# Input and latent weights of a hybrid attention block packed by K tile, multiplied K outermost over six feature tiles

## Chip, core and metric

The kernel runs on one core of a Trainium2 chip. The time is the device time of one execution in microseconds (us). Three timed runs of the kernel before took 450.87, 450.98 and 451.32 us; the median is 450.98 us.

## The reference

The block takes x with 256 positions and 1024 features, normalizes it, and multiplies it by one wide matrix `w_in`. The first 704 columns of `w_in` give the latents: 384 for the queries, 256 for keys and values, and 64 for a shared rotary key.

```python
h = rmsnorm(x, attn_norm[l])
proj = h @ w_in[l]
q_lat = proj[..., OFF_QLAT:OFF_KVLAT]
kv_lat = proj[..., OFF_KVLAT:OFF_KPE]
k_pe = proj[..., OFF_KPE:OFF_MOBA]
qkv_b = proj[..., OFF_MOBA:OFF_GATE]
gates = jax.nn.sigmoid(proj[..., OFF_GATE:] + b_gate[l])
```

Two attention branches follow (MLA from the latents, and MoBA from `qkv_b`, which for 256 positions is causal attention within one block). They are merged by the gates and projected. Then comes a gated feed-forward part with a short causal convolution, and a last norm. All of it is float32.

## The kernel before

The kernel makes every float32 product on TensorE of three float32r matmuls. Each operand is split into a part rounded to float32r (the high part, written by ScalarE) and the rest (the low part, written by VectorE), and the three are high by high, high by low and low by high (`mm3`, `split`). A matmul of a feature tile multiplies a 128x128 tile of weights by 256 positions.

The weights stream through SBUF once. `unit_plan` lists the loads in the order of their use; a unit is 128 partitions by 2048 float32, 1 MB. `weights` takes the next unit: a raw tile, a high tile and a low tile, each from a ring of three, the load on SyncE's queue (SP), and the split. The queue is in order: a load that waits for its raw tile holds up those behind it.

The order of instructions on each engine is set by a planner. All instructions are recorded in the order of the computation; `Program.emit` then gives each engine the oldest instruction whose operands are there by a simple model of times. Loads on SP keep their recorded order. What stands within `P.together()` stays together.

The first stage computes six feature tiles of 128 columns, the latents (the sixth is the rotary key, doubled). It goes like this:

- TensorE runs ten matmuls on a zeroed tile `warm`, and SP loads the input norm's weights `prm[:, :KT]`.
- The transposed input comes from its own array `xT` and unit `("lat", 0)`, two feature tiles, from `wpack`. Both are loaded in five pieces each, in turn: K tile 0, K tile 1, then 2 and 3, 4 and 5, 6 and 7. A piece of one K tile has 256 columns, 1 KB in a row.
- For each of the eight K tiles ScalarE scales and rounds the input (`XH`) and rounds the weights (`whi`), and VectorE writes the rests (`XL`, `wlo`), all 256 columns wide. TensorE multiplies K outermost over the two feature tiles, 6 matmuls a K tile, 48 in all.
- Units `("lat", 1)` and `("lat", 2)` follow in `proj_pair`: two feature tiles each, all K tiles of one tile and then of the next, 48 matmuls each. Each unit has its own PSUM bank of the ring `mm_bank` (three banks). Unit 1 is loaded in four pieces, unit 2 in two.
- After each unit, `keep_latents` copies its bank to SBUF and squares it, both on ScalarE.

The value projection of MoBA (`proj_tokens("v", 0, ...)`, units `v` 0 and 1) is the next work of TensorE, and then units `v` 2 and 3. Between the two the input is loaded again by rows (`b8`), and its norm's factor is worked out from it.

Of the kernel before, what the change touches and what calls it, by code (L numbers as in the profile page):

```python
"""Hybrid MLA + MoBA block with a ConvFFN on one core.

Every float32 product on the tensor engine is three float32r passes: both operands are split
into a part rounded to float32r and the exact rest (hi*hi + hi*lo + lo*hi, summed in PSUM).
Weights stream through SBUF once, in the order of their use, and are split on the way.
Activations stay on chip, features on partitions where they are contracted next.

MoBA: SEQ equals MOBA_BLOCK, so there is one block, none lies in the past of any query, every
selected score is masked and what is left is causal attention within the block.
"""  # L10
# [28 lines left out]
# columns of the small parameters  # L39
# [4 lines left out]
def unit_plan():  # L44
    """The weights in the order of their use: (kind, index)."""
    plan = [("lat", 0), ("lat", 1), ("lat", 2)]
# [17 lines left out]
SIZE = {"mqk": 3 * 384 + 2 * 256}  # the others have UNIT columns  # L64


def pack_weights(w_in, w_uq, w_ukv, w_o_mla, w_o_moba, w_out, w_up, w_down):
    """Layout alone: each unit as [128 rows of K, column group, K tile, columns of the group]."""
# [9 lines left out]
    # rotated halves lie 64 partitions apart: [x1, x1, x2, x2]  # L78
# [3 lines left out]
    for kind, i in PLAN:  # L82
        if kind == "lat":
            u = tiles(w_in, lat_cols[256 * i : 256 * i + 256], 128 if i else 256)
# [34 lines left out]
def rope_tables():  # L119
    """cos and the signed sin by [row, position]; rows r and r + 64 are a rotated pair."""  # L120
# [11 lines left out]
def constants():  # L132
    """Tables that depend on shapes alone: rope, the identity, the causal mask of a block, the
    rows of the first and of the second head in a pair's rotated tile."""
    p = np.arange(128)
    mask = np.where(p[None, :] <= p[:, None], 0.0, -1e30).astype(np.float32)
    sel = np.stack([(p // 32) % 2 == 0, (p // 32) % 2 == 1], axis=1).astype(np.float32)
    return np.ascontiguousarray(
        np.concatenate([*rope_tables(), np.eye(128, dtype=np.float32), mask, sel], axis=1)
    )  # L140


class Program:
    """Instructions, recorded in the order of the computation and emitted in the order of a
    simple model of the engines: each engine takes the oldest of its instructions whose operands
    are there. What reads or writes the same part of a tile keeps its order, and so do functions
    of the scalar engine with tables of their own."""

    LATENCY = {"tensor": 0.8}  # others 0.15
    DMA_LATENCY = 1.6  # L150

    def __init__(self, nc):
        self.nc = nc
        self.ops = []  # [engine, cost, calls, dependencies]
        self.users = {}  # tile -> [(op, region, writes)]
# [8 lines left out]
    def together(self):  # L164
        """Instructions of one engine that stay together."""
# [42 lines left out]
    def emit(self):  # L208
# [16 lines left out]
        for _ in range(n):  # L225
            best = None
            for e, js in open_ops.items():
                if not js:
                    continue
                if e == "sync":  # a queue  # L230
                    js = [j for j in js if j == min(loads)]
                    if not js:
                        continue
# [14 lines left out]
            else:  # L248
                free[e] = end = start + cost
            for a in after[j]:  # L250
# [19 lines left out]
def region(ap):  # L270
    """Partitions and elements of a tile that an access covers."""
# [5 lines left out]
def price(engine, method, args, kw):  # L277
    """Microseconds, about."""
    n = max(int(np.prod(a.shape[1:])) for a in list(args) + list(kw.values())
            if hasattr(a, "offset"))  # L280
    if engine == "tensor":
# [3 lines left out]
        return passes * max(0.107, 0.0025 + args[0].shape[1] / 2400)  # L285
    if engine == "scalar":
# [12 lines left out]
def hybrid_block(ctx: ExitStack, tc: tile.TileContext, xT, x, par, con, fnorm, wpack, out):  # L299
# [9 lines left out]
    class Ring:  # L309
        """Tiles that take turns."""  # L310
# [32 lines left out]
    units = iter(range(len(PLAN)))  # L343

    def weights(kind, i, *cuts):
        """The next unit's two parts, split in pieces that end at the cuts."""
# [5 lines left out]
        for a, b in zip((0, *cuts), cuts) if u < 3 else ((0, n),):  # L352
            sp.dma_start(raw[:, a:b], wpack[u, :, a:b])
# [22 lines left out]
    first = T("first", [4])  # L376
    act.activation(first, mhalf, AF.Exp)
    o = av_bank()
    for _ in range(10):
# [3 lines left out]
    sp.dma_start(prm[:, :KT], par[:, :KT])  # L383
    xraw, w0 = raws(), raws()
    wv = [his(), los()]
    next(units)
    xh, xl = T("XH", [KT, S], F32R), T("XL", [KT, S], F32R)
    for ks in ((0,), (1,), (2, 3), (4, 5), (6, 7)):
        c = slice(S * ks[0], S * ks[-1] + S)
        sp.dma_start(xraw[:, c], xT[:, c])  # L390
        sp.dma_start(w0[:, c], wpack[0, :, c])
    for k in range(KT):
        c = slice(S * k, S * k + S)
        g = prm[:, P_AN + k : P_AN + k + 1]
        act.activation(xh[:, k], xraw[:, c], AF.Copy, scale=g)
        act.copy(wv[0][:, c], w0[:, c])
        dve.scalar_tensor_tensor(xl[:, k], xraw[:, c], g, f32(xh[:, k]), op0=ALU.mult,
                                 op1=ALU.subtract)
# [506 lines left out]
```

## Time and profile before

| | |
|---|---|
| timed runs | 450.87, 450.98, 451.32 us, median 450.98 |
| span of the profiled execution | 450.0 us; its own time is not listed apart from the span |
| TensorE matmuls busy | 439.0 us (98%), 3302 |
| weight loads (PEld) | 415.4 us (92%) |
| VectorE | 356.7 us (79%) |
| ScalarE | 274.8 us (61%) |
| mean DMA rate over the span | 182 GB/s |
| TensorE's mean granted clock | 0.992 |

The span is the time from the first to the last instruction of the profiled execution. Times in rows of the trace are in us from its start. All instructions of the kernel go through a recorder and so bear its line (L242); a row is told apart by engine and by tiles, written as out<-in. `XH` and `XL` are the input's two parts, `whi` and `wlo` the weights', `raw` a loaded unit, `mm`, `av` and `sc` PSUM banks, `gate` the tile that holds the latents in the first stage, `warm` the zeroed tile.

### The profile page before, as it was taken

What the parts mean: (1) busy time and instruction counts of PE and PEld (TensorE: products, weight loads), DVE (VectorE), ACT (ScalarE), POOL (GpSimd) and SP (SyncE); (2) the same over time, 40 slices, a digit from 0 to 9 for tenths busy, and PEclk for the clock granted to TensorE, in tenths of its full rate; (3) what the DMA queues carried; (4) which work ended last, traced back from release to release, by engine and by line L of the source; (5) the groups of instructions that cost most, each with busy time, mean ns of one, the idle gap of its engine ahead of it and who ended that gap; (6) DMA issues with size and microseconds to landing.
All of it is one profiled execution on the core that took longest, in us unless ns stands there. A gap on an engine that the chain in (4) does not pass through costs nothing.

```text
span 450.0 us, 8134 instructions
## 1 busy us (share of the span) xinstructions
PE 439.0 (98%) x3302; PEld 415.4 (92%) x3302; DVE 356.7 (79%) x548; ACT 274.8 (61%) x475; POOL 10.8 (2%) x26
## 2 busy tenths in 40 slices
PE   7999999999999999999999999999999999999993
PEld 4988999999999999999998899999999999999982
DVE  3767998888987988793788568997887797797764
ACT  5786446546554766877765558765565565565523
POOL 0010300000000000000000010000000000000002
PEclk9999999999999999999999999999999999999998
DMA  6994745455254434240288454375555555556002
GB/s 197 399 402 162 263 155 184 178 183 181 90 185 165 137 124 182 93 174 17 105 340 302 188 188 137 144 288 197 190 201 203 192 205 198 197 192 233 2 1 93
DMA packets 13861, 81.77 MB, mean 182 GB/s; under 512 B 1664, under 2 KB 2560, under 8 KB 5120
## 3 DMA queue, kind: packets, MB, share of 16 engines
q1 hardware_dynamic: 13824, 81.25, 49.9%
q8 instruction: 26, 0.43, 0.4%
q14 instruction: 11, 0.09, 0.1%
HBM read 80.20 MB, written 1.05 MB: 181 GB/s over the span
## 4 chain that ended last, share of the span: by engine, by line
PE 96%; DMA 1%; SPq 1%; ACT 1%; POOL 1%; issue 0%; DVE 0%; POOLq 0%; ACTq 0%
PE mm L242 69%; PE av L242 14%; PE sc L242 12%; DMA raw<-in_wpack 1%; SPq L242 1%; POOL smalls L242 1%; ACT tb L242 0%; DVE gate L242 0%; ACT B L242 0%; POOLq L900 0%; ACT whi L242 0%; POOLq L242 0%; ACTq L242 0%
## 5 line engine op out<-in xcount | busy, mean ns | idle before, releaser
L242 ACT CAST whi<-raw 128x1024 fp32r<-128x1024 f32 (+3 forms) x158 | 152.3, 978 | 86.0 <-PE mm L242 70.3
L242 DVE TENSOR_TENSOR wlo<-raw,whi 128x1024 fp32r<-128x1024 f32 (+3 forms) x158 | 175.8, 1129 | 34.6 <-ACT whi L242 33.9
L242 PE MATMUL mm<-XH,whi 128*128 128x256 f32 x656 | 184.4, 281 | 1.8 <-ACT whi L242 1.8
L242 PE MATMUL mm<-XH,wlo 128*128 128x256 f32 x656 | 182.7, 278 | 0.0
L242 PE MATMUL mm<-XL,whi 128*128 128x256 f32 x656 | 182.5, 278 | 0.0
L242 PEld LDWEIGHTS mm<-XH,whi 128*128 128x128 f32 x656 | 124.3, 189 | 2.7 <-ACT whi L242 2.3
L242 PEld LDWEIGHTS mm<-XL,whi 128*128 128x128 f32 x656 | 124.2, 189 | 0.5
L242 PEld LDWEIGHTS mm<-XH,wlo 128*128 128x128 f32 x656 | 124.4, 190 | 0.2 <-DVE wlo L242 0.2
L242 DVE SCALAR_TENSOR_TENSOR tb<-ta,prm,tb 128x255 f32<-128x255 f32 x88 | 40.4, 480 | 2.2 <-ACT tb L242 0.7
L242 ACT ACTIVATE tb<-ta,prm 128x256 f32<-128x256 f32 x44 | 24.3, 595 | 3.8 <-DVE ta L242 3.8
L242 ACT ACTIVATE e<-sc,smalls 128x128 f32<-128x128 f32 (+1 forms) x32 | 13.3, 419 | 12.6 <-DVE smalls L242 11.7
L242 DVE TENSOR_TENSOR ta<-ta,tb 128x256 f32<-128x256 f32 (+1 forms) x35 | 16.9, 484 | 2.2 <-ACT ta L242 0.7
L242 ACT CAST qh<-ta 128x256 fp32r<-128x256 f32 (+1 forms) x26 | 11.4, 437 | 11.8 <-DVE ta L242 11.7
L242 DVE TENSOR_TENSOR ta<-mm,rbc 128x512 f32<-128x512 f32 x22 | 15.2, 689 | 4.2 <-PE mm L242 4.2
L242 PE MATMUL mm<-YBH,whi 128*128 128x256 f32 x64 | 18.1, 283 | 0.0
L242 PE MATMUL mm<-YBH,wlo 128*128 128x256 f32 x64 | 17.7, 277 | 0.0
L242 PE MATMUL mm<-VH,whi 128*128 128x256 f32 x64 | 17.7, 277 | 0.0
L242 PE MATMUL mm<-YBL,whi 128*128 128x256 f32 x64 | 17.7, 277 | 0.0
L242 PE MATMUL mm<-VL,whi 128*128 128x256 f32 x64 | 17.7, 276 | 0.0
L242 PE MATMUL mm<-VH,wlo 128*128 128x256 f32 x64 | 17.7, 276 | 0.0
L242 PE MATMUL sc<-whi,ql 128*128 128x512 f32 x44 | 17.3, 394 | 0.0
L242 PE MATMUL av<-whi,ql 128*128 128x512 f32 x44 | 17.3, 394 | 0.0
(167 smaller groups left out, 735.1 us busy)
## 6 DMA issues: line engine op xcount, KB each, us to landing
raw<-in_wpack SPq DMA_DIRECT2D x66, 1024.0 KB, 4.8
raw<-in_wpack SPq DMA_DIRECT2D x4, 832.0 KB, 4.2
raw<-in_wpack SPq DMA_DIRECT2D x7, 256.0 KB, 6.6
raw<-in_wpack SPq DMA_DIRECT2D x2, 512.0 KB, 5.2
B<-in_x SPq DMA_DIRECT2D x1, 1024.0 KB, 10.0
gate<-in_x SPq DMA_DIRECT2D x1, 1024.0 KB, 4.8
raw<-in_xT SPq DMA_DIRECT2D x3, 256.0 KB, 6.1
cst<-in_con SPq DMA_DIRECT2D x1, 641.0 KB, 11.1
```

Source lines behind the costliest of these rows:

```text
L242: getattr(getattr(self.nc, e), method)(*args, **kw)
```

## The change

The transposed input and the latents' weights are packed together by K tile. Units `("lat", 0..2)` and the array `xT` give way to four units `("first", 0..3)`. Each holds two K tiles, and of each K tile 256 columns of input and then 768 columns of weights, so that a K tile is 4 KB of a row. The bytes are the same, 4 MB. Each of the four is loaded in two pieces of one K tile; in the first unit the first piece is cut once more, into the input with two feature tiles and the other four feature tiles.

TensorE multiplies K outermost over all six feature tiles: 18 matmuls a K tile, in three banks of `mm_bank`, 144 matmuls as before. The latents are kept after the last K tile, all three banks one after the other. The weights of a K tile are split 768 columns at once, but for K tile 0, which is split as 256 and 512; the first 256 are rounded on VectorE. The ten warming matmuls are seven. The load of `prm[:, :KT]` moves from SP's queue to ScalarE's, ahead of ScalarE's first activation. The planner gets a price for such a load. Comments and docstrings are blanked, which changes no instruction.

```diff
-    plan = [("lat", 0), ("lat", 1), ("lat", 2)]
+    plan = [("first", j) for j in range(KT // 2)]
...
-        if kind == "lat":
-            u = tiles(w_in, lat_cols[256 * i : 256 * i + 256], 128 if i else 256)
+        if kind == "first":
+            rows = [slice(128 * k, 128 * k + 128) for k in (2 * i, 2 * i + 1)]
+            u = np.concatenate([t for r_ in rows for t in (xT[r_], w_in[r_][:, lat_cols])], axis=1)
...
                 free[e] = end = start + cost
+                if calls[0][1] == "dma_start":
+                    end += self.DMA_LATENCY
...
+    if method == "dma_start" and engine != "sync":
+        return 0.06
...
-        for a, b in zip((0, *cuts), cuts) if u < 3 else ((0, n),):
-            sp.dma_start(raw[:, a:b], wpack[u, :, a:b])
+        sp.dma_start(raw[:, :n], wpack[u, :, :n])
...
+    o = av_bank()
+    for _ in range(7):
+        mm(o, warm[:, 0:128], warm, True, True)
+
+    prm = T("prm", [NPAR])
+    act.dma_start(prm[:, :KT], par[:, :KT])
     first = T("first", [4])
     act.activation(first, mhalf, AF.Exp)
-    o = av_bank()
-    for _ in range(10):
-        mm(o, warm[:, 0:128], warm, True, True)
-
-    prm = T("prm", [NPAR])
-    sp.dma_start(prm[:, :KT], par[:, :KT])
-    xraw, w0 = raws(), raws()
-    wv = [his(), los()]
-    next(units)
     xh, xl = T("XH", [KT, S], F32R), T("XL", [KT, S], F32R)
-    for ks in ((0,), (1,), (2, 3), (4, 5), (6, 7)):
-        c = slice(S * ks[0], S * ks[-1] + S)
-        sp.dma_start(xraw[:, c], xT[:, c])
-        sp.dma_start(w0[:, c], wpack[0, :, c])
-    for k in range(KT):
-        c = slice(S * k, S * k + S)
-        g = prm[:, P_AN + k : P_AN + k + 1]
-        act.activation(xh[:, k], xraw[:, c], AF.Copy, scale=g)
-        act.copy(wv[0][:, c], w0[:, c])
-        dve.scalar_tensor_tensor(xl[:, k], xraw[:, c], g, f32(xh[:, k]), op0=ALU.mult,
-                                 op1=ALU.subtract)
-        dve.tensor_sub(wv[1][:, c], w0[:, c], f32(wv[0][:, c]))
-    w0 = [t.rearrange("p (k c) -> p k c", c=256) for t in wv]
+    def first_unit(j):
+        u = next(units)
+        assert PLAN[u] == ("first", j)
+        raw, hi, lo = raws(), his(), los()
+        for a, b in ((0, 512), (512, 1024), (1024, 2048)) if j == 0 else ((0, 1024), (1024, 2048)):
+            sp.dma_start(raw[:, a:b], wpack[u, :, a:b])
+        for kk in range(2):
+            k, c, w = 2 * j + kk, 1024 * kk, 768 * kk
+            g = prm[:, P_AN + k : P_AN + k + 1]
+            x = raw[:, c : c + S]
+            act.activation(xh[:, k], x, AF.Copy, scale=g)
+            for i, (a, b) in enumerate(((0, 256), (256, 768)) if k == 0 else ((0, 768),)):
+                src = raw[:, c + S + a : c + S + b]
+                if k == 0 and i == 0:
+                    dve.tensor_copy(hi[:, w + a : w + b], src)
+                else:
+                    act.copy(hi[:, w + a : w + b], src)
+                if i == 0:
+                    dve.scalar_tensor_tensor(xl[:, k], x, g, f32(xh[:, k]), op0=ALU.mult,
+                                             op1=ALU.subtract)
+                dve.tensor_sub(lo[:, w + a : w + b], src, f32(hi[:, w + a : w + b]))
+        return [t[:, : 2 * 768].rearrange("p (k m c) -> p k m c", m=6, c=128) for t in (hi, lo)]
...
-    o = mm_bank()
-    for k in range(KT):
-        for m in range(2):
-            with P.together():
-                feature_tile(o, m, [t[:, :, 128 * m : 128 * m + 128] for t in w0], xh, xl, [k],
-                             k == 0 and m == 0, k == KT - 1)
-    keep_latents(o, 0, 2)
-    o = proj_pair("lat", 1, xh, xl, 512, 1024, 1536, 2048)
+    banks = [mm_bank() for _ in range(3)]
+    for j in range(KT // 2):
+        wv = first_unit(j)
+        for kk in range(2):
+            k = 2 * j + kk
+            for m in range(6):
+                with P.together():
+                    mm3(banks[m // 2][:, S * (m % 2) : S * (m % 2) + S], wv[0][:, kk, m],
+                        wv[1][:, kk, m], xh[:, k], xl[:, k], k == 0 and m % 2 == 0, k == KT - 1)
     sp.dma_start(prm[:, KT:], par[:, KT:])
-    keep_latents(o, 2, 2)
-    lat2 = proj_pair("lat", 2, xh, xl)
-    keep_latents(lat2, 4, 1)
+    for f, o in enumerate(banks):
+        keep_latents(o, 2 * f, 1 + (f < 2))
+    lat2 = banks[2]
```

## Rows read from the trace of the kernel before

**Rows 1.** The chain that ended last, share of the span by engine.

```profile
PE 96%; DMA 1%; SPq 1%; ACT 1%; POOL 1%; issue 0%; DVE 0%; POOLq 0%; ACTq 0%
```

**Rows 2.** Waits of PE in the whole span: total us, times, longest.

```profile
PE mm L242 <- ACT whi L242: 1.8, 1, 1.8
PE av L242 <- POOL mhalf L242: 1.3, 1, 1.3
```

**Rows 3.** The chain that ended last, in time: start us, us, what.

```profile
3.52 5.26 DMA raw<-in_wpack
...
9.25 17.06 PE mm L242 x132
26.31 10.99 PE av L242 x48
```

**Rows 4.** Timeline of PE at the start: start us, us, instruction, count.

```profile
1.29 4.45 PE L242 MATMUL av<-warm 128*128 128x512 bf16 x10 [1.29 <-POOL mhalf L242]
5.18 0.77 PE L242 MATMUL mm<-XH,whi 128*128 128x256 f32 x1
...
5.97 0.41 PE L242 MATMUL mm<-XH,wlo 128*128 128x256 f32 x1
6.18 0.34 PE L242 MATMUL mm<-XH,whi 128*128 128x256 f32 x1
...
7.16 0.28 PE L242 MATMUL mm<-XH,wlo 128*128 128x256 f32 x1
```

**Rows 5.** Windows: length, PE, PEld, DVE, ACT, POOL busy, clock, DMA share, GB/s.

```profile
7.30:9.25 1.95, 0.14 (x2) 0.00 (x0) 0.90 (x3) 1.30 (x4) 0.00 (x0) 1.00 0.78 200
9.25:13.10 3.85, 3.85 (x18) 3.69 (x19) 3.15 (x9) 3.20 (x10) 0.00 (x0) 0.56 1.04 387
13.10:26.30 13.20, 13.20 (x117) 13.20 (x117) 9.71 (x13) 10.32 (x14) 0.00 (x0) 1.00 1.02 405
26.30:37.30 11.00, 11.00 (x51) 9.03 (x50) 5.72 (x8) 6.74 (x14) 1.28 (x4) 1.00 0.83 328
```

**Rows 6.** Timeline of SP's queue at the start.

```profile
0.72 0.38 SPq L242 DMA_DIRECT2D prm<-in_par  x1
1.16 0.42 SPq L242 DMA_DIRECT2D raw<-in_xT  x1
1.63 0.42 SPq L242 DMA_DIRECT2D raw<-in_wpack  x1
```

**Rows 7.** Timeline of ScalarE (ACT).

```profile
4.04 0.51 ACT L242 ACTIVATE XH<-raw,prm 128x256 fp32r<-128x256 f32 x1 [1.83 <-DMA raw<-in_xT]
...
8.79 0.71 ACT L242 CAST whi<-raw 128x256 fp32r<-128x256 f32 x2 [0.65 <-DMA raw<-in_wpack]
...
30.70 2.00 ACT L242 CAST whi<-raw 128x1024 fp32r<-128x1024 f32 x2 [1.25 <-DMA raw<-in_wpack]
```

**Rows 8.** Timeline of VectorE (DVE).

```profile
4.58 0.48 DVE L242 SCALAR_TENSOR_TENSOR XL<-raw,prm,XH 128x256 fp32r<-128x256 f32 x1 [4.58 <-ACT XH L242]
4.98 0.42 DVE L242 TENSOR_TENSOR wlo<-raw,whi 128x256 fp32r<-128x256 f32 x1
```

**Rows 9.** Groups by form: busy us, mean ns of one, idle before.

```profile
L242 DVE TENSOR_TENSOR wlo<-raw,whi 128x768 fp32r<-128x768 f32 x4 | 3.8, 951 | 0.0
L242 ACT ACTIVATE XH<-raw,prm 128x256 fp32r<-128x256 f32 x8 | 3.7, 501 | 4.1 <-DMA raw<-in_xT 4.1
L242 DVE SCALAR_TENSOR_TENSOR XL<-raw,prm,XH 128x256 fp32r<-128x256 f32 x8 | 3.6, 482 | 6.8 <-ACT XH L242 6.8
L242 ACT CAST whi<-raw 128x768 fp32r<-128x768 f32 x4 | 3.4, 839 | 0.0
L242 ACT ACTIVATE gate<-mm 128x512 f32<-128x512 f32 x2 | 1.2, 606 | 0.0
L242 ACT COPY gate<-mm 128x512 f32<-128x512 f32 x2 | 1.2, 588 | 1.8 <-PE mm L242 1.8
```

**Rows 10.** DMA issues: count, KB each, median us to landing.

```profile
raw<-in_wpack SPq DMA_DIRECT2D x66, 1024.0 KB, 4.8
raw<-in_xT SPq DMA_DIRECT2D x2, 128.0 KB, 2.9
prm<-in_par SPq DMA_DIRECT2D x1, 4.0 KB, 1.8
```

More of the change, by code (lines that the diff above doesn't have):

```diff
@@ L64, with pack_weights @@
 SIZE = {"mqk": 3 * 384 + 2 * 256}
-def pack_weights(w_in, w_uq, w_ukv, w_o_mla, w_o_moba, w_out, w_up, w_down):
+def pack_weights(xT, w_in, w_uq, w_ukv, w_o_mla, w_o_moba, w_out, w_up, w_down):
     def tiles(w, cols, group):
@@ L298, in hybrid_block @@
 @with_exitstack
-def hybrid_block(ctx: ExitStack, tc: tile.TileContext, xT, x, par, con, fnorm, wpack, out):
+def hybrid_block(ctx: ExitStack, tc: tile.TileContext, x, par, con, fnorm, wpack, out):
     ctx.enter_context(tc.manual_schedule())
@@ L886 @@
     arrays = {
-        "xT": xs.T.reshape(KT, 128, S).transpose(1, 0, 2).reshape(128, KT * S),
         "x": xs.reshape(2, 128, D).transpose(1, 0, 2),
@@ L891 @@
         "fnorm": a["final_norm"],
-        "wpack": pack_weights(*(a[n][0] for n in ("w_in", "w_uq", "w_ukv", "w_o_mla", "w_o_moba",
+        "wpack": pack_weights(xs.T, *(a[n][0] for n in ("w_in", "w_uq", "w_ukv", "w_o_mla", "w_o_moba",
                                                   "w_out", "w_up", "w_down"))),
```

## The prediction

> **What bounds the kernel now.** I read the chain of waits first. TensorE (PE) is 96% of the chain that ended last [rows 1], so the time is what TensorE takes, plus what stands ahead of its first product and behind its last. Next come its own waits: in the whole span there are two, 1.3 us for the zeroed tile at the start and 1.8 us for a rounded weight tile [rows 2]. The chain in order of time puts the second: it runs over a load issued at 3.52 that lands at 8.78, goes to 132 products from 9.25 to 26.31, and from there on to the values' products [rows 3]. So everything that could be won here lies before 26.31, the end of the latents' 144 matmuls, and from 26.31 on TensorE never waits for another engine.
>
> What does that stretch cost? At full clock 117 matmuls start within 13.20 us [rows 5], 0.113 us each; 144 of them are 16.3 us. The first starts at 5.18 [rows 4], so the ideal end is 21.5, and 4.8 us are lost. The timeline and the windows show where. The first products run 0.21 us apart (5.97 to 6.18), then twelve are done and nothing follows 7.16 until 9.25 [rows 3, 4]. After that idle stretch the granted clock is 0.56 of full over 9.25 to 13.10, where 18 matmuls start in 3.85 us instead of 34 [rows 5]; that is the half level, 1.2 of 2.4 GHz, nearly throughout, and costs 16 x 0.113 = 1.8 us. The wait is for data: 12 matmuls use up two K tiles, 512 KB, and the next 512 KB (two pieces of 256 KB) land only at 8.79 [rows 7], with 200 GB/s in 7.30 to 9.25 against 387 and 405 GB/s afterwards [rows 5].
>
> **The change part by part.** Matmuls, bytes and the elements that are split are the same in number. What moves is how much TensorE has to do for each byte that has landed. Before, 256 KB of input and weights feed 6 matmuls (0.68 us at full clock) and later units alone catch up. Afterwards 512 KB feed 18 matmuls, 2.03 us. At 387 GB/s [rows 5] 512 KB take 1.35 us, so once running the loads are ahead of TensorE by 0.7 us a K tile.
>
> *First product.* SP issues its small load at 0.72 and the first piece of input at 1.16 [rows 6]. With the small load on ScalarE's queue the first piece goes out at 0.72. The 128 KB piece was in use at 4.04, 2.88 after its issue [rows 6, 7]; the new one has 128 KB more, 0.3 to 0.65 us at 405 to 200 GB/s [rows 5]. I take 0.4, so ScalarE starts at 4.0, as before. The small load is then late by nothing: it took 1.8 us from issue [rows 10] and would land near 2.5; behind it on ScalarE wait only its table load and a first activation, done long before 4.0. First product: input rounded by 4.5, so 4.6. VectorE's rounding of the first 256 weight columns has no row; between nothing and the 0.42 us of a same-sized subtraction [rows 8] it ends by 4.5 and is hidden beside ScalarE. The rest of the weights is at hand at 5.4, as in the profile (4.98 + 0.42) [rows 8]; the third product waits for it. Seven warming matmuls, 0.43 us apart, end at 4.3; ten end at about 5.7, later than the first product's operands, so three fewer free TensorE in time and leave it idle for about 0.3 us.
>
> *K tile 0.* Two products run by 5.0, sixteen are left at 5.4. The other four feature tiles (second piece, issued 0.47 later by the spacing of SP's issues [rows 6]) land near 4.5 and are split by about 6.0 at 0.5 to 0.7 us on each engine, ahead of the seventh product. At 0.113 us TensorE is through at 7.2, at 0.21 us at 8.8. In the profile the clock rose at about 6.2, with TensorE busy from 1.29 [rows 4]. Afterwards it is busy but for 0.3 us at 4.3 and 0.4 us at 5.0; I take the same rise and so about 7.4.
>
> *K tile 1.* This one decides. It is 512 KB in one piece, issued third, at 1.66. By then 1 MB has to come. One-megabyte loads take 4.8 us from issue to landing (median of 66) [rows 10]; from the second issue at 1.19 that is 6.0. From below: a 128 KB piece took 2.9 us [rows 10], which gives 4.6. From above: the profile's own fourth K tile, at the same 1 MB, was there at 8.79 [rows 7]. I take 6.0, nearest to the many loads, as the packets are now 4 KB where they were 1 and 2 KB. Then input 0.50, 768 columns of weights 0.84 on ScalarE and 0.95 on VectorE [rows 9], and about 0.1 between: the last operand at 8.4. TensorE does two products meanwhile and idles for roughly 0.8 us. Against the 1.9 us now, the wait is shorter and the clock should hold.
>
> *K tiles 2 to 7.* ScalarE needs 0.50 + 0.84 = 1.34 us, VectorE 0.48 + 0.95 = 1.43 us [rows 9], the loads 1.35 us, TensorE 2.03: TensorE is last from here. The fourth unit's load waits for the first raw tile, free at about 8.4, with 2 MB still in the queue ahead of it; it is needed at 18. Of the 144 products 20 are done at 8.4; 124 x 0.113 = 14.0, so the latents end at 22.4.
>
> *Bank switches.* TensorE now changes the bank every three or six products. The values' products alternate between two banks every three matmuls, and there TensorE is busy for 11.00 of 11.00 us at clock 1.00 [rows 5]: cost nothing. The Trainium skill speaks against this edit (TensorE: Matmul & The Clock Gate, section "A second HAM failure mode: psum-queue depth-cycling"): cycling through banks lets TensorE pause between groups until its clock swings between the levels. The row of the values' products does not show it; if it came, it would be a case of its own, below.
>
> *Keeping the latents.* Three banks are kept at once at 22.4: two copies and two squares of 512 columns at 0.59 and 0.61 [rows 9] and two of 256 at no more than that, at most 3.6 us on ScalarE in one lump, where a third of it stood at the end before. Behind it wait the squares for the input's norm and the split of the third value unit. That unit's split started at landing, 30.70 [rows 7], and would be needed 3.9 us earlier than 37.30, at 33.4; its first half, 1.0 on ScalarE and 1.2 on VectorE, is ready at 32.9 even if the load is no earlier, and with a shorter stall at 7 to 9 it is. So nothing, and 1 to 2 us at most if both go wrong.
>
> **Sum.** 26.31 - 22.4 = 3.9 us earlier, and TensorE carries that through, since it waits for nothing behind. The span goes from 450.0 to 446.1. The timed median lies 0.98 above the span; with the same 0.98 the time is 447.1.
>
> **Rivals.** *Second K tile and clock later than taken, gain halved.* If the idle bits of the first 6 us keep the clock low until 9.7, 24 products are done then and 120 x 0.113 = 13.6 end at 23.3; with a landing at 7.0 on top, 24.2. Gain 2 to 3 us, 448 to 449. For it: the rate was still 200 GB/s in 7.30 to 9.25 [rows 5], behind where this load falls. Against it: rows of 1 and 2 KB were moved there, and the gap in TensorE's work is shorter.
>
> *No change.* The slow stretch from 7.30 to 9.25 belongs to the time, not to the small pieces: then 1 MB lands at 8.8 as now, the last operand of K tile 1 comes at 11.2, and at full clock the latents end at 11.2 + 14.0 = 25.2; with the clock low to 13.1, as now, at 26.2. Time 450 to 451. For it: the same load sizes flowed at 387 GB/s right after, so size alone doesn't explain the dip. Against: 256 KB pieces alternated between two arrays there.
>
> *Slower.* The same late K tile with a low clock that holds on. Its place is the gap between K tile 0 and 1, now filled by two products, after which TensorE idles from 7.4 to 10 and again to 11.2, longer than the profile's 1.9 us. Each us at half clock costs 0.5. It decides from 4 us at half clock after 11.2, which eat the 1.1 us of the 25.2 case and 0.9 more; at 5.3 us the latents end at 27.8, and the time is 452.5. For it: 3.85 us at 0.56 followed the idle stretch now [rows 5]. The Trainium skill's rule bears on this (same page, section "Loop structure matters more than you think"): a long load wait in front of each K tile's matmuls drops the clock. Against: K tiles 2 to 7 are paced by TensorE in every version of the loads.
>
> *Clock swings with the banks.* If half of the 124 products ran at 0.21, 62 x 0.1 = 6.2 us would be lost, and the time would be 453.3.
>
> **How the numbers follow.** Forecast 0.64, halved gain 0.18, no change 0.09, slower 0.07, swings 0.02. The forecast's own range: a landing at 4.6 makes K tile 0 the bound (18 products by 7.2 and 126 x 0.113 = 14.2: 21.4), a gain of 4.9 and 446.1; a landing at 7.0 gives 448.1. The range takes the halved gain and most of no change: 445.9 to 450.4; some 0.14 lies above, 0.04 below. Less than 0.2% (0.9 us) can't be told from no change here. Faster: forecast and halved gain, 0.82; same 0.09; slower 0.09.
>
> **What would show it.** Right: one wait of TensorE under 1 us near 8, no stretch at half clock behind 9.7, latents' products ending near 22.4, values' products right behind them, and the rest shifted as a whole. Wrong at the first step: first product past 5.2. Wrong at K tile 1: landing past 7. Wrong in the sum: TensorE waits behind 26 us that are not there now, above all for the value units' splits behind the kept latents.

## The result and the profile after

Four timed runs of the changed kernel took 448.12 to 449.55 us, median 448.58; four of the kernel before, timed with them, 450.87 to 451.52, median 451.15. The ratio is 0.9935, 95% interval 0.9914 to 0.9956: 2.57 us faster, where 447.1 us and a gain of 3.9 were forecast. The profiled execution took 448.98 us, its span is 447.2, where that of before was 450.0. Executions of one kernel differ: of 25 of the kernel before on the chip of e5 to e8, the 14 with a mean granted clock of 0.994 or more had a median of 451.22 us, the other 11 of 452.96, so a median also tells in how many of them the clock was low.

In the rows of after all recorded instructions bear L243. First the waits of TensorE over the whole span (total us, times, longest), which answer to [rows 2]: the wait of 1.8 us for a rounded weight tile is gone. In its place stand two for VectorE's rests, 0.7 us in all. The last two lines were not there before and count 0.2 us each; the one for `diag` stands at 49.1, behind the latents.

```profile
PE av L243 <- POOL mhalf L243: 1.3, 1, 1.3
PE mm L243 <- DVE wlo L243: 0.7, 2, 0.5
PE sc L243 <- DVE diag L243: 0.2, 1, 0.2
PE mm L243 <- ACT XH L243: 0.2, 1, 0.2
```

The chain that ended last, in time (start us, us, what), against [rows 3]. It runs over a load that lands at 8.42, K tile 2's, and goes to TensorE at 10.72 for the last 106 of the latents' products. The values' products begin at 23.48 in the chain, where they began at 26.31: 2.83 us earlier.

```profile
2.08 6.34 DMA raw<-in_wpack
...
10.72 12.75 PE mm L243 x106
23.48 11.20 PE av L243 x48
```

TensorE's timeline (start us, us, instruction, count, [idle before <-releaser]) gives the same stretch product by product, against [rows 4]. The first product starts at 4.63. K tile 0's products run through, and twenty are done when the first stop comes, from 7.39 to 8.16, for K tile 1's last operand. The second stop is from 10.21 to 10.72, for K tile 2's.

```profile
1.29 3.17 PE L243 MATMUL av<-warm 128*128 128x512 bf16 x7 [1.29 <-POOL mhalf L243]
4.63 0.38 PE L243 MATMUL mm<-XH,whi 128*128 128x256 f32 x1 [0.17 <-ACT XH L243]
...
7.39 0.28 PE L243 MATMUL mm<-XL,whi 128*128 128x256 f32 x1
8.16 0.38 PE L243 MATMUL mm<-XH,wlo 128*128 128x256 f32 x1 [0.49 <-DVE wlo L243]
...
9.88 0.28 PE L243 MATMUL mm<-XL,whi 128*128 128x256 f32 x1
9.99 0.28 PE L243 MATMUL mm<-XH,wlo 128*128 128x256 f32 x1
10.10 0.28 PE L243 MATMUL mm<-XH,whi 128*128 128x256 f32 x1
10.21 0.28 PE L243 MATMUL mm<-XL,whi 128*128 128x256 f32 x1
10.72 0.39 PE L243 MATMUL mm<-XH,wlo 128*128 128x256 f32 x1 [0.23 <-DVE wlo L243]
...
11.42 0.28 PE L243 MATMUL mm<-XL,whi 128*128 128x256 f32 x1
11.54 0.28 PE L243 MATMUL mm<-XH,wlo 128*128 128x256 f32 x1
11.65 0.28 PE L243 MATMUL mm<-XH,whi 128*128 128x256 f32 x1
11.77 0.28 PE L243 MATMUL mm<-XL,whi 128*128 128x256 f32 x1
```

ScalarE's timeline shows the landings, since its scaling of a K tile (`XH`) starts when the piece is there; it answers to [rows 7]. At 4.07 it had waited for the small load, not for the input. K tile 1 was there at 5.88. K tile 2 came only at 8.45, 2.57 us later, and K tile 3 was there by 9.69, 1.24 after that.

```profile
4.07 0.51 ACT L243 ACTIVATE XH<-raw,prm 128x256 fp32r<-128x256 f32 x1 [1.43 <-DMA prm<-in_par]
...
5.88 0.51 ACT L243 ACTIVATE XH<-raw,prm 128x256 fp32r<-128x256 f32 x1 [0.75 <-DMA raw<-in_wpack]
...
8.45 0.51 ACT L243 ACTIVATE XH<-raw,prm 128x256 fp32r<-128x256 f32 x1 [1.33 <-DMA raw<-in_wpack]
...
9.69 0.51 ACT L243 ACTIVATE XH<-raw,prm 128x256 fp32r<-128x256 f32 x1
```

The windows (length, busy time of each engine, granted clock, DMA share, GB/s) stand against [rows 5]. From 4.63 to 7.39 the rate is 283 GB/s, from then on 391 to 410. No stretch is at half clock behind 4.63.

```profile
4.63:7.39 2.76, 2.62 (x19) 2.43 (x20) 1.88 (x5) 1.73 (x3) 0.00 (x0) 1.00 0.94 283
7.39:10.72 3.33, 2.61 (x20) 2.21 (x19) 2.21 (x4) 2.26 (x4) 0.00 (x0) 1.00 1.01 410
10.72:23.48 12.76, 12.76 (x107) 12.76 (x108) 8.99 (x13) 8.53 (x14) 0.00 (x0) 1.00 1.01 398
14.00:23.00 9.00, 9.00 (x79) 9.00 (x78) 5.45 (x7) 4.92 (x8) 0.00 (x0) 1.00 1.00 391
```

The start of the same product in order in both traces says where the time comes from. The table was read from the starts of TensorE's products, the warming ones left out (us from the span's start):

| product | before | after | difference |
|---|---|---|---|
| 0, the first | 5.18 | 4.63 | -0.55 |
| 12 | 9.25 | 6.53 | -2.72 |
| 36 | 13.91 | 10.10 | -3.81 |
| 48 | 15.27 | 12.01 | -3.26 |
| 144, the first of the values | 26.15 | 23.31 | -2.84 |
| 192 | 37.13 | 34.52 | -2.61 |
| 264 | 50.89 | 48.28 | -2.62 |
| 276 | 52.25 | 50.12 | -2.13 |
| 300 | 55.04 | 52.85 | -2.19 |
| 500 | 78.56 | 75.54 | -3.02 |
| the last | 441.74 | 438.71 | -3.03 |

The gain is made in the first 36 products: 2.2 us in the stop that before had at product 12, another 1.1 while before ran at half clock (less the first stop of after). 0.55 goes at K tile 2's stop. Three things move the difference behind product 48. The wider spacing of products at full clock in after (last section) takes 0.65 up to product 192. The wait for VectorE's `diag` at 49.1 costs 0.5 by starts, between products 264 and 276; `diag` came at 49.04 in this execution, at 48.44 in that of e9, which has no such wait. And before has a stretch of the wider spacing of its own, from product 300 on, which gives 0.9 back by product 500.

### The profile page after: what moved, and what is told of

Same layout as the page of the kernel before. It is cut to its first block, busy times and chain, and to the rows that moved or that the text cites. A ratio compares the mean times of both kernels' runs of the same rounds, so it can differ in the third digit from the quotient of the medians.

```text
span 447.2 us, 8109 instructions
## 1 busy us (share of the span) xinstructions
PE 436.6 (98%) x3299; PEld 412.6 (92%) x3299; DVE 356.7 (80%) x544; ACT 273.3 (61%) x469; POOL 11.6 (3%) x26
## 4 chain that ended last, share of the span: by engine, by line
PE 92%; DVE 2%; DMA 1%; POOL 1%; ACT 1%; issue 1%; SPq 0%; POOLq 0%; ACTq 0%
PE mm L243 66%; PE av L243 14%; PE sc L243 12%; DMA raw<-in_wpack 1%; DVE wlo L243 1%; POOL smalls L243 1%; ACT tb L243 0%; DVE VL L243 0%; SPq L243 0%; DVE gate L243 0%; DVE tb L243 0%; ACT whi L243 0%; ACT B L243 0%; POOLq L913 0%; DVE diag L243 0%
## 5 line engine op out<-in xcount | busy, mean ns | idle before, releaser
L243 DVE TENSOR_TENSOR wlo<-raw,whi 128x1024 fp32r<-128x1024 f32 (+3 forms) x153 | 175.7, 1162 | 35.2 <-ACT whi L243 34.5
L243 ACT CAST whi<-raw 128x1024 fp32r<-128x1024 f32 (+3 forms) x152 | 151.2, 1008 | 84.1 <-PE mm L243 67.4
L243 PE MATMUL mm<-XH,whi 128*128 128x256 f32 x656 | 183.2, 279 | 0.2 <-ACT XH L243 0.2
L243 PE MATMUL mm<-XH,wlo 128*128 128x256 f32 x656 | 181.7, 277 | 0.7 <-DVE wlo L243 0.7
L243 PE MATMUL mm<-XL,whi 128*128 128x256 f32 x656 | 181.6, 277 | 0.1
L243 PEld LDWEIGHTS mm<-XH,whi 128*128 128x128 f32 x656 | 123.2, 188 | 1.5 <-ACT XH L243 1.1
L243 PEld LDWEIGHTS mm<-XH,wlo 128*128 128x128 f32 x656 | 123.2, 188 | 1.1 <-DVE wlo L243 1.1
L243 PEld LDWEIGHTS mm<-XL,whi 128*128 128x128 f32 x656 | 123.4, 188 | 0.8 <-DVE XL L243 0.3
L243 DVE SCALAR_TENSOR_TENSOR tb<-ta,prm,tb 128x255 f32<-128x255 f32 x88 | 40.5, 481 | 2.2 <-ACT tb L243 0.7
L243 ACT ACTIVATE tb<-ta,prm 128x256 f32<-128x256 f32 x44 | 24.2, 595 | 3.8 <-DVE ta L243 3.8
L243 ACT ACTIVATE e<-sc,smalls 128x128 f32<-128x128 f32 (+1 forms) x32 | 13.3, 419 | 12.8 <-DVE smalls L243 11.9
L243 ACT CAST qh<-ta 128x256 fp32r<-128x256 f32 (+1 forms) x26 | 11.4, 437 | 12.3 <-DVE ta L243 12.2
L243 DVE TENSOR_TENSOR ta<-ta,tb 128x256 f32<-128x256 f32 (+1 forms) x35 | 16.9, 484 | 2.2 <-ACT ta L243 0.7
L243 DVE TENSOR_TENSOR ta<-mm,rbc 128x512 f32<-128x512 f32 x22 | 15.2, 690 | 4.2 <-PE mm L243 4.2
L243 PE MATMUL mm<-YBH,whi 128*128 128x256 f32 x64 | 18.1, 283 | 0.0
L243 PE MATMUL mm<-YBH,wlo 128*128 128x256 f32 x64 | 17.7, 277 | 0.0
L243 PE MATMUL mm<-VH,whi 128*128 128x256 f32 x64 | 17.7, 277 | 0.0
L243 PE MATMUL mm<-YBL,whi 128*128 128x256 f32 x64 | 17.7, 277 | 0.0
L243 PE MATMUL mm<-VH,wlo 128*128 128x256 f32 x64 | 17.7, 276 | 0.0
L243 PE MATMUL mm<-VL,whi 128*128 128x256 f32 x64 | 17.7, 276 | 0.0
L243 PE MATMUL sc<-whi,ql 128*128 128x512 f32 x44 | 17.3, 394 | 0.0
L243 PE MATMUL av<-whi,ql 128*128 128x512 f32 x44 | 17.3, 394 | 0.0
```

Of the source, the lines that this page charges most:

```text
L243: getattr(getattr(self.nc, e), method)(*args, **kw)
```

## The experiments

The theory: TensorE gains because a landed byte now feeds more products, so it neither runs dry nor loses its clock in the first 15 us. The rivals: the gain is the earlier start (first piece, small load, seven warming products), or the wider rows, and the order has no part in it. All but e11 were timed against the kernel before on their chip; its median there was 451.38 us for e1 to e4, 451.76 for e5 to e8, 451.75 for e12, 452.24 for e9 to e11. Where times from two chips are compared, the differences to the kernel before on each chip are the safer numbers.

**e1, the small load back on SP's queue.**

```diff
-    act.dma_start(prm[:, :KT], par[:, :KT])
+    sp.dma_start(prm[:, :KT], par[:, :KT])
```

> The changed kernel with the small load of the norm's weights back on SP's queue, ahead of the first piece. Theory A (the path of the start runs through the first pieces' issue): the first piece goes out at 1.15 instead of 0.72, but the small load lands near 2.5 instead of 4.05; the first scaling of the input starts near 4.3 instead of 4.07, K tiles 1 and 2 land 0.45 later, and the values' products begin at 23.5 to 23.8 instead of 23.31: the time is 0.2 to 0.5 us above the changed kernel, 448.8 to 449.1. Theory B (the move is hidden behind the later landing of K tile 2 anyway): values' products at 23.2 to 23.4, time unchanged within 0.2 us.

Measured: 451.86 us, ratio 1.0021 (1.0002 to 1.0041). Both theories missed: the whole gain is gone. ScalarE's and TensorE's timelines of e1 show two things. K tile 1 was there at 8.40 instead of 5.88; and the products of K tile 0 start 0.21 us apart, not 0.113, and go on so until 13.8, where the granted clock rises.

```profile
8.40 0.51 ACT L243 ACTIVATE XH<-raw,prm 128x256 fp32r<-128x256 f32 x1 [2.49 <-DMA raw<-in_wpack]
```

```profile
8.14 0.41 PE L243 MATMUL mm<-XH,wlo 128*128 128x256 f32 x1
8.35 0.41 PE L243 MATMUL mm<-XH,whi 128*128 128x256 f32 x1
...
13.62 0.38 PE L243 MATMUL mm<-XH,whi 128*128 128x256 f32 x1
13.84 0.28 PE L243 MATMUL mm<-XL,whi 128*128 128x256 f32 x1
13.96 0.28 PE L243 MATMUL mm<-XH,wlo 128*128 128x256 f32 x1
```

**e2, ten warming products.**

```diff
-    for _ in range(7):
+    for _ in range(10):
```

> The changed kernel with ten warming matmuls again. Theory A (K tile 1 decides): TensorE's first product starts near 5.55 instead of 4.63, but its eighteen products of K tile 0 still end before K tile 1's last operand at 8.11, so the values' products begin at 23.3 as before and the time is the same within 0.3 us. Theory B (the earlier first product is a gain of its own): everything is 0.9 us later, 449.5.

Measured: 448.6 us, ratio 0.9943 (0.9926 to 0.996), as the changed kernel. First product 0.55 us later, first values' product at 22.92, 0.39 earlier than in the trace of after. The three products taken away bring nothing here.

**e3, pieces of 2 KB rows.** K tiles loaded in two pieces each.

```diff
-        for a, b in ((0, 512), (512, 1024), (1024, 2048)) if j == 0 else ((0, 1024), (1024, 2048)):
+        for a, b in ((0, 512), (512, 1024), (1024, 1536), (1536, 2048)):
```

> The changed kernel with every K tile loaded in two pieces of 2 KB rows, instead of one piece of 4 KB rows from K tile 1 on. Theory A (the order of the products is what counts; the rows only through SP's issues, 0.47 us each): K tile 1's second piece is issued at 2.1 instead of 1.62 and K tile 2's at 3.1 instead of 2.08; the values' products begin 0.3 to 1.0 us later, at 23.6 to 24.3, time 448.9 to 449.6, still 1.5 us or more below the kernel before. Theory B (wide rows make the gain): K tile 2 lands past 10 us instead of 8.42, the values' products begin past 25, time 450.3 or more.

Measured: 449.21 us, ratio 0.9951 (0.9931 to 0.9971); K tile 1's second half landed at 6.27, K tile 2's at 9.08, the first values' product started at 23.12. The width of the rows is worth at most the 0.6 us between the medians, and the intervals don't tell even that from nothing. The rival that the widest rows make the gain falls; rows of 1 KB, which before had in its first two K tiles, were not tried.

**e4, the old order recorded.** The loads as changed, but the products recorded two feature tiles at a time over all K tiles.

```diff
-    for j in range(KT // 2):
-        wv = first_unit(j)
...
+    wvs = [first_unit(j) for j in range(KT // 2)]
+    for ms in ((0, 1), (2, 3), (4, 5)):
+        for k in range(KT):
...
```

> The changed kernel with the same loads and splits, but the products in the order of the kernel before: two feature tiles over all K tiles, then the next two, then the last two (the fourth unit's two parts stand in the values' tiles, which are idle then). Theory A (the gain is the order): the first pair follows the K tiles' landing and ends behind the last operand of K tile 7 near 17.1 us; 96 products of 0.113 to 0.118 follow, so the values' products begin at 28.0 to 28.6, the span is 451.5 to 452.5 and the time 452.8 to 454, above the kernel before. Theory B (the gain is the packing and the earlier, wider loads): values' products at 23.3 to 25, time 450 or less, below the kernel before.

Measured: 449.42 us, ratio 0.9962 (0.9943 to 0.998). This didn't test what it should: the planner takes the oldest product whose operands are there, so it filled the gaps with the later feature tiles, and 144 products ran through from 4.73. The order in the text is not the order on the engine.

**e5, e1 with ten warming products.** The edits of e1 and e2 together. The small load and the warming are those of the kernel before; the packing, the order and the wider splits that go with them differ.

> The small load on SP's queue ahead of the first piece, as in e1, and ten warming matmuls instead of seven. In e1 K tile 1 landed at 8.38 instead of 5.86 and the clock stayed at half until 13.83. Theory A (both counted in e1): the ten matmuls keep TensorE busy to 5.5 and through K tile 0, the clock is full before 8, but K tile 1's last operand still comes near 10.7; the values' products begin at 24.7 to 25.4 and the time is 449.8 to 450.7, between e1's 451.9 and the changed kernel's 448.6. Theory B (the low clock was all of e1's loss): 448.4 to 449.2. Theory C (the late K tile was all of it): 451.4 or more.

Measured: 449.48 us, ratio 0.9952 (0.9925 to 0.9979). K tile 1 is as late as in e1 (8.45), but the clock was full from 5.28 on. One window of e1 and of e5 shows what that is worth: 33 products against 49 in the same 8.53 us. (The clock column shows nothing ahead of the first change that a trace records, so e1's 1.00 up to 13.83 isn't to be read; the spacing tells.)

```profile
5.30:13.83 8.53, 7.84 (x33) 7.16 (x34) 5.34 (x9) 5.88 (x10) 0.00 (x0) 1.00 0.99 373
```

```profile
5.30:13.83 8.53, 6.49 (x49) 5.66 (x48) 5.27 (x9) 5.81 (x10) 0.00 (x0) 1.00 0.98 370
```

Against the kernel before on its own chip e1 stands 0.5 us above, e5 2.3 below and e2, with the small load moved and ten warming products, 2.8 below. So of e1's 3.3 us the clock brings back 2.8, and 0.5 is left for the late K tile. The traces divide it otherwise: the first values' product starts at 26.32 in e1, 24.93 in e5 and 22.92 in e2, which is 1.4 for the clock and 2.0 for the K tile. And e5's ten executions lie between 448.19 and 452.28 us, the quickest as quick as e2's. Both count; how the loss divides is not settled. The packing, with its order and splits, is worth 2.3 us (451.76 to 449.48), if the clock rises.

**e6, the kernel before with its small load moved.** Nothing else of the change.

```diff
+    prm = T("prm", [NPAR])
+    act.dma_start(prm[:, :KT], par[:, :KT])
     first = T("first", [4])
...
-    prm = T("prm", [NPAR])
-    sp.dma_start(prm[:, :KT], par[:, :KT])
```

> The kernel before with one part of the change alone: its small load on ScalarE's queue ahead of the first activation, so that the first piece of the input is issued at 0.72 instead of 1.16. Theory A (what decides is whether the early pieces land before the slow stretch of the loads at about 5 to 8 us): the pieces of K tiles 2 and 3 land well over 0.45 us earlier than 8.79, TensorE's wait of 1.8 us shrinks below 1 and the time falls to 449.6 or less. Theory B (each piece is 0.45 us earlier and no more, 6 products a K tile still starve TensorE): the wait stays above 1.3 us, the time is 450.4 to 451.2.

Measured: 450.54 us, ratio 0.9974 (0.9956 to 0.9992), 1.2 us faster: the time and the wait are theory B's, the landing is theory A's. The pair of pieces that came at 8.79 in [rows 7] landed at 7.69. TensorE waits as long as before, but in two stops, and the clock stays full from 5.21 on, where it fell to half in [rows 5]:

```profile
PE mm L242 <- ACT whi L242: 1.8, 2, 1.2
```

**e7, the old order enforced.** As e4, with the planner bound to the recorded order for these 144 products (the parts of the fourth unit lie in the values' tiles, as all four units must now be held).

```diff
+                if e == "tensor" and self.strict:
+                    js = [j for j in js if j == min(self.strict)]
...
+    P.strict = {n for n in range(start, len(P.ops)) if P.ops[n][0] == "tensor"}
```

> As e4 (two feature tiles over all K tiles, then the next two), but with the planner held to that order for the 144 products; in e4 it had filled the waits of the first pair with products of the other pairs, so that the order was hardly undone. Theory A (the gain needs all six feature tiles of a K tile to be multiplied when it lands): the first pair ends behind the last operand of K tile 7 near 17.1 us, 96 products at 0.113 to 0.118 follow, values' products at 28.0 to 28.6, span 451.5 to 452.5, time 452.8 to 454. Theory B (the loads alone make the gain): 449.4, as e4.

Measured: 455.59 us, ratio 1.0086 (1.0059 to 1.0114), 3.8 us slower than the kernel before on that chip; the changed kernel, in its own runs, was 2.6 faster than before. The pieces land as in after (K tile 1 at 6.03), but TensorE has six products for each of them; its products run 0.21 us apart until 14.8, and the first values' product starts at 30.50. Its waits and, from its chain, the last stretch:

```profile
PE mm L249 <- ACT XH L249: 4.3, 1, 4.3
PE mm L249 <- ACT whi L249: 1.3, 2, 1.0
PE mm L249 <- DVE VL L249: 0.6, 2, 0.3
PE mm L249 <- DVE wlo L249: 0.4, 2, 0.2
```

```profile
17.22 12.10 PE mm L249 x100
```

The edit does one thing more than the text above says. The planner holds back every other instruction of TensorE until the 144 products are placed, so the seven warming products come behind them: TensorE stands idle to 4.35 (the wait of 4.3) and starts with a low clock, and warming products lie between the last latents' product at 29.04 and the first of the values at 30.50, which costs 1.3 us. The low clock does not decide the rest, since TensorE waits at full clock for the low part (`VL`) of K tile 7's weights and goes on with it only at 17.22. At that time 100 of the 144 products are left, where in after about 50 are. Without the 1.3 us the values would begin at 29.2, an estimate, still 3.0 behind before (26.15) and 5.9 behind after (23.31). So with the same pieces in the same queue, the old order makes the kernel slower than before. That is the theory's central point; the loss beyond what it had expected is mostly the misplaced warming.

**e8, the first piece held back.** VectorE writes into the piece's place first, so SP issues it at 1.41 instead of 0.72; the small load still goes at 0.71.

```diff
+        if j == 0:
+            dve.memset(raw[:, 0:512], 0.0)
```

> The changed kernel with its first piece held back by a memset of that raw tile on VectorE, so that it is issued at about 1.1 instead of 0.72, as in e1, while the small load stays on ScalarE's queue. Theory A (0.4 us of issue is what makes K tile 1 fall into the slow stretch): K tile 1 lands past 7.5, time 450.5 or more. Theory B (the small load's packets ahead of the pieces in SP's own queue did it): K tile 1 lands near 6.3, time 448.8 to 449.4.

Measured: 450.93 us, ratio 0.9977 (0.9955 to 0.9999). 0.69 us of delay cost 2.35 us by the medians, 1.7 by the differences to before. K tile 1 landed at 9.20. The ten executions lie between 448.5 and 452.18 us, so not all of them need have done the same. The profiled one, 452.06 us and among the longest, fell back to half clock from 7.68 to 14.51:

```profile
4.30:7.68 3.38, 2.32 (x13) 1.59 (x12) 1.64 (x4) 1.03 (x2) 0.00 (x0) 1.00 0.65 205
7.68:14.51 6.83, 5.49 (x25) 4.91 (x24) 4.51 (x8) 5.11 (x9) 0.00 (x0) 0.50 1.01 407
```

**e9, the changed kernel again, unedited.**

> The changed kernel once more, for its time on the same chip as the next run and for a second trace. If the landing of K tile 1 near 5.9 and of K tile 2 near 8.4 belongs to the kernel and not to one execution, both come within 0.4 us of that again, and the ratio to the kernel before is within 0.992 to 0.996. If it was luck, K tile 1 lands past 7 in this trace and the ratio is above 0.996.

Measured: 448.39 us, ratio 0.9913 (0.9893 to 0.9933). K tile 1 landed at 6.43, 0.6 later than in after, and the ratio lies just below the range; both expected bounds were missed narrowly. Still, an early landing was seen in both executions that were traced. In this one the clock was low until 9.69. It had no stop at K tile 2, because TensorE was later there, and the chain has all 144 products in one piece:

```profile
4.79 19.07 PE mm L243 x144
23.86 10.99 PE av L243 x48
```

**e10, K tiles 1 and 2 split as 256 and 512 columns**, so that TensorE can begin on them earlier.

```diff
-            for i, (a, b) in enumerate(((0, 256), (256, 768)) if k == 0 else ((0, 768),)):
+            for i, (a, b) in enumerate(((0, 256), (256, 768)) if k < 3 else ((0, 768),)):
```

> The changed kernel with the weights of K tiles 1 and 2 split as 256 and 512 columns instead of 768, as those of K tile 0 are. Theory A (TensorE waits for the low part of all 768 columns): the first 256 columns of K tile 1 are ready at about 7.2 instead of 8.11 and those of K tile 2 at about 9.8 instead of 10.68; the wait before K tile 1 goes, the one before K tile 2 stays under 0.6 us, the values' products begin at 22.2 to 22.7 instead of 23.31 and the time is 0.6 to 1.1 us below the changed kernel's. Theory B (the landing is what counts, or the two more splits push the later ones back): within 0.3 us of it.

Measured: 448.35 us, ratio 0.9923 (0.9906 to 0.9941), beside 448.39 for e9 on the same chip. Neither stop is in its list of waits any more, though at K tile 1, which landed at 6.47, TensorE still loses some 0.7 us by starts. The first values' product starts at 22.41, 0.90 us earlier than in after; 0.33 of that is after's wider spacing behind product 48. Yet the timed median is the same, as theory B had it. A reading that no run tests: what a stop costs depends on whether the clock had risen by then, and e9 shows that it hadn't always. It is no better version.

**e11, the loads of the pieces held back by 4.5 us**, timed once.

```diff
+        if j == 0:
+            for _ in range(2):
+                dve.memset(raw, 0.0)
```

> The changed kernel with its first piece held back by two long memsets of that raw tile on VectorE, to about 4.6 instead of 0.72: only for what the loads do, the time is some 3 to 4 us longer. In all runs the loads flow at 250 to 300 GB/s from about 5 to 7.5 and above 370 afterwards. Theory A (the slow stretch hangs on the time since the program's start): K tile 2 lands within 1.5 us of K tile 1, since both come after 8. Theory B (it hangs on what the loads themselves have done, a given time or number of bytes after their own start): the slow stretch lies at 9 to 11.5, K tile 1 lands near 9.8 and K tile 2 2.2 us or more behind it.

Measured: 453.96 us. The first piece was issued at 5.26, K tile 1 landed at 12.63, 7.37 later, K tile 2 only 1.26 behind it, which is the sign that was named for theory A. The rate says otherwise: it is low at 9.76 to 11.76, long after it had risen in after.

```profile
9.76:11.76 2.00, 2.00 (x12) 2.00 (x11) 0.69 (x1) 0.06 (x1) 0.00 (x0) 1.00 0.89 274
```

So the slow stretch goes with the start of the loads and not with the time since the program's start, as theory B had it, though B's landings were not met either: the stretch was over before K tile 1 was there, and so K tile 2 came close behind.

**e12, e8 with the small load held back too.** Both are issued at 1.4, as they are both at 0.7 in the changed kernel.

```diff
+    dve.memset(raws.tiles[0][:, 0:512], 0.0)
+    dve.memset(prm[:, :KT], 0.0)
     act.dma_start(prm[:, :KT], par[:, :KT])
```

> The changed kernel with both the first piece and the small load held back by about 0.7 us, by two writes of VectorE into their tiles, so that both are issued near 1.4 to 1.5 us and the small load is again in flight on ScalarE's queue beside the first piece; e8 held the first piece back alone. Theory A (the small load in flight on the other queue beside the first piece is what lets K tile 1 land early): K tile 1's last landing comes within 6.2 us of the first piece's issue, near 6.7 to 7.6, and the time is 448.6 to 449.6 us. Theory B (the later start itself is what makes K tile 1 late, and the small load is a bystander): K tile 1 lands 7.2 us or more after that issue, at 8.6 or later, and the time is as in e8, 450.5 us or more.

Measured: 448.9 us, ratio 0.9938 (0.9914 to 0.9962). K tile 1 landed at 6.69, 5.28 after the first piece's issue: theory A, in landing and in time. The rows of e8 and then of e12, from SP's, ScalarE's and its queue's timelines and from one window: the same issue of the first piece, the small load 0.73 later, K tile 1 2.51 earlier, and 324 GB/s where e8 has 96.

```profile
0.71 0.38 ACTq L243 DMA_DIRECT2D prm<-in_par  x1
1.41 3.49 SPq L243 DMA_DIRECT2D raw<-in_wpack  x7
...
9.22 0.51 ACT L243 ACTIVATE XH<-raw,prm 128x256 fp32r<-128x256 f32 x1 [2.79 <-DMA raw<-in_wpack]
...
3.91:4.91 1.00, 0.67 (x3) 0.15 (x1) 0.74 (x3) 0.51 (x1) 0.00 (x0) 1.00 0.53 96
```

```profile
1.41 7.89 SPq L243 DMA_DIRECT2D raw<-in_wpack  x9
1.44 0.39 ACTq L243 DMA_DIRECT2D prm<-in_par  x1
...
6.71 0.51 ACT L243 ACTIVATE XH<-raw,prm 128x256 fp32r<-128x256 f32 x1 [1.04 <-DMA raw<-in_wpack]
...
3.91:4.91 1.00, 0.41 (x2) 0.00 (x0) 0.52 (x2) 0.26 (x1) 0.00 (x0) 1.00 0.90 324
```

Over all runs with the new packing, K tile 1's landing less the first piece's issue falls into two groups, with one traced execution for each entry:

| small load | runs: landing less issue, us |
|---|---|
| issued on ScalarE's queue beside the first piece | after 5.14, e2 5.19, e12 5.28, e7 5.31, e3 5.55, e9 5.71, e10 5.75, e4 6.13 |
| issued 0.4 to 4.6 us ahead of it, on SP's queue (e1, e5) or ScalarE's | e1 7.23, e5 7.30, e11 7.37, e8 7.79 |

## Why the prediction was right, and where it was too large

*The mechanism.* Right, and shown: TensorE's stop at 7.16 to 9.25 with the half clock behind it was the cost [rows 3 to 5], and more products for a landed byte take it away. e7 undoes this and is slower than before, also without its misplaced warming; e5, with the small load and the warming of before, still has 2.3 us; e6 keeps the stop of before at full clock and has 1.2.

*First product and K tile 0.* 4.6 was forecast and 4.63 measured; through at 7.4 and measured 7.2. But the clock was full from 4.6 on, not from 6.2, and ScalarE's start was set by the small load (landed at 4.05, 3.3 us after issue, not near 2.5) and not by the piece (3.86).

*The small load's move.* "Late by nothing" was right in its price and wrong in its weight. Without it and with seven warming products there is no gain at all (e1), with ten there is (e5), and with it even the old kernel is 1.2 us faster (e6). The issue 0.44 us earlier is not the reason, as e12 starts 0.7 later and keeps nearly everything. The page that bears on this is "DMA: Bandwidth & Descriptors" of the Trainium skill, section "Issuing engines are not separate DMA queues": issuing from several engines at once saves only the time of the issue. This case does not agree: the move brought the issue of K tile 1 forward by 0.46 us, from 2.08 in e1 to 1.62 in after, and its landing by 2.52, from 8.38 to 5.86.

*K tile 1.* Landing 6.0 and last operand 8.4 were forecast; it was 5.86 and 8.11. The wait of "roughly 0.8 us" was 0.49 in the waits, or 0.66 by starts (0.77 between 7.39 and 8.16, less one product). The landing was met in part by luck: 6.0 was taken from the 1 MB loads and the packets of 4 KB, but rows of half the width land nearly as early (6.27 in e3), and with the small load on SP's queue the same piece landed at 8.38 (e1), close to the 8.8 of the case "no change".

*K tiles 2 to 7.* Here the sum was mis-sized. "TensorE is last from here" took the loads 1.35 apart from K tile 1 on. K tile 2 came 2.56 later, because the slow stretch of the loads (283 GB/s over 4.63 to 7.39) came ahead of it. From 8.16 to the first values' product there are 124 products in 15.15 us, where 124 x 0.113 is 14.0: 0.40 is the second stop, about 0.24 the slow first product behind each of the two stops, and 0.5 the spacing of 0.118 us. The earlier operand gives 0.24 back. So the latents' products ended at 23.3 and not at 22.4.

*The sum.* 3.9 took 26.31 for the end of before, the chain's value, while 22.4 counts starts; by starts it is 26.15 and 3.75. Of that 0.9 went as above. "TensorE carries that through" did not hold in this execution: 0.2 went in the wider spacing of the values' products and 0.5 in the wait for `diag` at 49.1, one of the waits behind 26 us that were named as a sign of an error. The trace of before then lost 0.9 in its own wider spacing, which is luck for the difference, so the end of TensorE moved by 3.03 us. The span moved by 2.8 and the medians by 2.57. The 0.98 between span and median joined two different executions: in 30 executions of before with e1 the median difference of time and span is 1.8, and 1.78 in the profiled one of after. So the profiled execution of before took some 451.8, an estimate, and was longer than its median.

*The rival "gain halved"* named 448 to 449 us, where the time lies, for a landing at 7.0 with a clock low until 9.7. The profiled execution had neither. e9 had the second and came out at 448.54: with a low clock to 9.7 TensorE is late enough to meet no stop at K tile 2, so both ways cost about the same.

*What was cost at nothing.* Keeping the latents took ScalarE from 22.10 to 24.7, and no wait of TensorE for ScalarE follows behind it; what makes `diag` late at 49.1 was not tested. The bank switches made no stretch at half clock: the granted clock is 1.00 over 10.72 to 23.48. The swing of the clock that the Trainium skill reports for cycling through banks (TensorE: Matmul & The Clock Gate, section "A second HAM failure mode: psum-queue depth-cycling") does not show here.

## What to carry to other kernels

Where loads bound the first microseconds, pack so that each landed piece feeds every product that can use it, and make the order on the engine, not the order in the text, show it. Read a stop of TensorE together with the clock behind it: against e2, the same late piece put the first values' product 2.0 us back with the clock up (e5) and 3.4 with it down (e1). An edit that is "free" in the sum still belongs in an experiment by itself when it sits ahead of everything.

## What had not been expected of the hardware

*Loads after their start.* In all twelve runs with the new packing the rate is 246 to 297 GB/s from 4.5 to 6.5 us after the first piece's issue, and 385 to 423 from 7.5 to 10.5 after it. What separates the two groups of the table lies ahead of that, from 2.5 to 3.5 us after the issue: 279 to 354 GB/s in the eight early runs, 96 to 168 in the four late ones. So the late K tile 1 is not caught by a slow stretch that has moved, but by a lull that the others do not have. The lull goes with how the small load is issued (table above). Why is open. In every run ScalarE's table load stands right behind the place of the small load, so it moves along with it, and no run has separated the two.

*Two spacings at full clock.* Products of 256 columns start 0.113 us apart in some stretches and 0.118 in others, at a granted clock of 1.00 in both: in after 79 of them are in flight at some time in 14:23, in before 82 in the same window, and there it is 79 in 54:63 (after: 82).

```profile
14.00:23.00 9.00, 9.00 (x82) 9.00 (x81) 5.51 (x9) 6.54 (x11) 0.00 (x0) 1.00 1.02 398
54.00:63.00 9.00, 9.00 (x79) 9.00 (x78) 8.91 (x13) 4.95 (x5) 0.00 (x0) 1.00 0.33 118
```

With 512 columns it is 0.233 and 0.229; the 48 values' products take 11.20 us in after and 10.99 in before and in e9. After has the wider spacing from about 11 to 35 us, before from about 53 to 80, e9 in neither stretch: its values' products start 0.39 us later than in after, and its last product 0.31 earlier. So it belongs to the execution and not to the kernel. What sets it off was not found.
